# Half of layer 1's modulation by VectorE instead of TensorE, partial sums in a slot

## The chip, the cores and the metric

The kernel runs on one core of one Trainium2 chip. The metric is the device time of one execution in microseconds; where several runs are given, their median.

## The reference

Two layers of a hybrid trunk run over 128 context tokens and 512 latent tokens with 1024 channels, all in fp32. Each layer is a gated feed-forward half-step, a mixer (windowed attention, pooling, short convolution) and a second feed-forward half-step; every one of the three starts from a modulated norm and ends with a gate. Shift, scale and gate of all three come from the modulation:

```python
def ada_params(cond, w_ada, b_ada):
    m = jax.nn.silu(cond) @ w_ada + b_ada          # 1024 -> 9 x 1024, for each layer
    return m.reshape(m.shape[:-1] + (N_MOD, D_MODEL))

def modulated_norm(x, mod, k, g):
    shift, scale = mod[:, None, 3 * k], mod[:, None, 3 * k + 1]
    return rms_norm(x, g) * (1 + scale) + shift

def ffn_sublayer(x, mod, k, g, w_in, w_out):
    h = modulated_norm(x, mod, k, g)
    gt, up = jnp.split(h @ w_in, 2, axis=-1)
    return x + 0.5 * mod[:, None, 3 * k + 2] * ((jax.nn.silu(gt) * up) @ w_out)
```

There are two condition vectors, one for latent and one for context tokens, so a layer's modulation is a product of 2 x 1024 with 1024 x 9216: few operations, but 36 MB of weights for each layer.

## The kernel before, in words

Activations are kept transposed, channels on partitions: eight tiles `xT` of 128 x 640 tokens, treated in two halves of 320. Every big product is done in three matmuls (`mm3`, lines 352 to 354): weights and activations are split into a rounded high part and a remainder (fp32r), and high x high, high x low and low x high are summed in PSUM. The six stages follow one another: (layer, sublayer) = (0, 0), (0, 1), (0, 2), (1, 0), (1, 1), (1, 2); sublayers 0 and 2 are feed-forward (`ffn`), 1 is the mixer.

A feed-forward stage runs over 22 tiles j of 128 hidden channels. Stage (0, 0) uses the plain form (`up`). Stages (0, 2), (1, 0) and (1, 2) use from j = 3 on the fast form (`fast_ups`, `fast_ends`): gate and up products in seven smaller products, numbered 1 to 7, of 12 matmuls each, in the order 1, then 3 and 4 of the j before, then 6, 2, 7, 5. Product 2 alone goes to the PSUM tile `po`. Product 7 of j starts the PSUM tile `c`; VectorE adds it to `gate2` (line 675), and product 4 of the same j, issued within the next j, then accumulates onto `c`. The weights for that are prepared in `fast_weights`: four additions by VectorE (line 646, into the two `sums` tiles) and four splits, each a copy by ScalarE (`wh`, line 170) and a subtraction by VectorE (`wl`, line 176). After j = 6, 11 and 15 a `down` multiplies a chunk of hidden tiles `g` by the second matrix; the last chunks follow after the loop.

All weights come through a ring of five tiles `raw` of 512 KB, loaded in order by SyncE's queue (SP). The tiles of the activations (`h`, `g` and others) are taken from one pool of 22 slots.

The modulation is done beside the feed-forward stages, in 18 chunks of 512 columns for each layer. `side` (line 1286), called after each j, advances a generator `ada_steps(l, c, vector)` by a number of steps that `spread` works out; a chunk has five steps, the first four each with a load of 512 KB of `w_ada` into a `raw` tile, the last with the closing work. `budget` (line 1335) gives 14 chunks (4 to 17 of layer 0) to stage (0, 0), 11 chunks (0 to 10 of layer 1) to (0, 2) and 7 chunks (11 to 17 of layer 1) to (1, 0). So stage (0, 2) does 55 steps over 20 values of j, (1, 0) does 35 over 20.

`ada_steps` has two ways. With `vector` false, each step issues 8 matmuls (`ada_matmuls`, line 275) with the condition in 32 columns as weights and 128 x 128 of `w_ada` as moving data, four column strips side by side; the PSUM tile `mis` is held for all five steps. With `vector` true, each step multiplies the loaded rows by the condition as a per-partition scalar and adds them up on VectorE (lines 309 and 311), for two conditions; at the end 8 matmuls with `pick` (line 319) add over the partitions. Both end with `add_bias`: a copy to `arow` by VectorE (line 264), a transpose by TensorE (line 265) and an addition (line 266). Before, `vector` is true for all of stage (0, 0) and false elsewhere.

The order on each engine's queue is laid out at build time by a planner, which takes the ready instruction of highest priority, where priority follows the order of the program, and gives out buffers as they come free. On the chip each engine runs its queue in that order.

Of the kernel before, what the change touches and what calls it, by code (L numbers as in the profile page):

```python
# [96 lines left out]
def trunk_kernel(ctx: ExitStack, tc: tile.TileContext, i: dict, o: dict):  # L97
# [16 lines left out]
    def mis():  # L114
        return mis_p.tile([P, 512], F32, tag="mis", name="mis")

    def slot(dt=F32, name="slot", shape=(2, T)):
        return slots.tile([P, *shape], dt, tag="slot", name=name)
# [23 lines left out]
    def raw_tile():  # L142
        return rawp.tile([P, 1024], F32, tag="raw", name="raw")

    def sum_tile(name="sums"):
        return sump.tile([P, 1024], F32, tag="sums", name=name)

    def load_ada(l, ci, q, tile):
        src = i["w_ada"][l, q * 256 : (q + 1) * 256, ci * 512 : (ci + 1) * 512]
        nc.sync.dma_start(tile, src.rearrange("(k p) c -> p k c", p=P))  # L150
        return tile
# [110 lines left out]
    def add_bias(l, ci, ps, row):  # L262

        nc.vector.tensor_copy(row, ps[:, 0:P])
        nc.tensor.transpose(ps[:, P : 2 * P], row, ident)
        nc.vector.tensor_tensor(
            mods[l][:, ci * 4 : ci * 4 + 4, :],
            ps[:, P : 2 * P].rearrange("p (g j) -> p g j", g=4)[:, :, 0:2],
            bcol[l][:, ci * 4 : ci * 4 + 4].unsqueeze(2).to_broadcast([P, 4, 2]),
            op=ALU.add,  # L270
        )

    def ada_matmuls(ps, r, q, k):
        for g in range(4):
            last = nc.tensor.matmul(  # L275
                ps[32 * g : 32 * g + 32, 0:P],
                c2[:, 2 * q + k, :],
                r[:, k, g * P : (g + 1) * P],
                start=(q + k == 0),
                stop=(q + k == 4),  # L280
            )
        return last
# [10 lines left out]
    def ada_steps(l, ci, vector):  # L293

        row = lambda: small.tile([P, P], F32, tag="sq", name="arow", bufs=3)
        if vector:
            part = sum_tile().rearrange("p (j c) -> p j c", j=2)
        else:
            ps = mis()
        for q in range(4):  # L300
            r = load_ada(l, ci, q, raw_tile().rearrange("p (k c) -> p k c", k=2))
            for k in range(2):
                if not vector:
                    ada_matmuls(ps, r, q, k)
                    continue
                for j in range(2):
                    c = c2[:, 2 * q + k, j : j + 1]
                    if q + k == 0:
                        nc.vector.tensor_scalar_mul(part[:, j, :], r[:, k, :], c)
                    else:  # L310
                        nc.vector.scalar_tensor_tensor(  # L311
                            part[:, j, :], r[:, k, :], c, part[:, j, :], op0=ALU.mult, op1=ALU.add
                        )
            yield
        if vector:
            ps = mis()
            for j in range(2):
                for g in range(4):
                    nc.tensor.matmul(
                        ps[32 * g : 32 * g + 32, 0:P],  # L320
                        pick[:, j, :],
                        part[:, j, g * P : (g + 1) * P],
                        start=(j == 0),
                        stop=(j == 1),
                    )
        add_bias(l, ci, ps, row())
# [4 lines left out]
    def gain(l, n, half):  # L331

        if half == 0:
            gains[l][n] = const.tile([P, KD, 2], F32, name=f"gain{l}{n}")
        a = gains[l][n][:, half * 4 : half * 4 + 4, :]
        c = (3 * n + 1) * 8 + half * 4
        g = gcol[:, (l * 3 + n) * 8 + half * 4 : (l * 3 + n) * 8 + half * 4 + 4]
        nc.vector.scalar_tensor_tensor(
            a, mods[l][:, c : c + 4, :], 1.0, g.unsqueeze(2).to_broadcast([P, 4, 2]), op0=ALU.add, op1=ALU.mult
        )  # L340

    def gate(l, n):
        g = mods[l][:, (3 * n + 2) * 8 : (3 * n + 3) * 8, :]
        if n != 1:
            t = const.tile([P, KD, 2], F32, name=f"gate{l}{n}")
            nc.vector.tensor_scalar_mul(t, g, 0.5)
            g = t
        gates[l][n] = g
# [23 lines left out]
    def norm_head(hf):  # L372
        a, b = HALVES[hf]
        ps = mis()
        nc.tensor.matmul(ps[:, :HALF], ones, ssq[:, a:b], start=True, stop=True)
        return rsqrt_newton(ps[:, :HALF], eps_d)
# [173 lines left out]
    def shift_products(gate, up):  # L550
# [3 lines left out]
        return bias, last  # L554

    def ffn(l, f, n, hs, side, finish, nxt, first=None):
        w_in = i["w_ffn_in"][l, f]
        w_out = i["w_ffn_out"][l, f]
# [151 lines left out]
        if first:  # L710
            first(gated)
        else:
            ups_by_half(0, 2)
            side(1)
        for j in range(2, NJ):
            if first or j < PLAIN:
                up(j)
            else:
                ends = fast_ups(j, ends)
            side(j)  # L720
            if ch < len(FF_CHUNKS) - 2 and j == FF_CHUNKS[ch][1] + (2 if first else 1):
                down(ch)
                ch += 1
# [15 lines left out]
    def load_mixer_constants():  # L739
        nc.sync.dma_start(edge, i["edge"].rearrange("p (t e) -> p t e", t=2))  # L740
        nc.sync.dma_start(pair, i["pair"])
        nc.sync.dma_start(sinkb, i["sink"].unsqueeze(0).to_broadcast([P, DEPTH, NH]))
        bcol.append(load_rows(72, (nc.sync, slice(0, 72), i["b_ada"][1].rearrange("(r c) -> r c", c=P))))
        gains_qk = [(nc.sync, (slice(16 + x, 18 + x), slice(h * HD, h * HD + HD)), i[w])
                    for x, w in ((0, "q_norm_g"), (2, "k_norm_g")) for h in range(2)]
        c = load_rows(
            20,
            (nc.sync, slice(0, 4), i["pool_scale"].rearrange("l (t p) -> (l t) p", p=P)),
            (nc.sync, slice(4, 16), i["conv_w"].rearrange("l k (t p) -> (l k t) p", p=P)),
            *gains_qk,  # L750
        )

        nc.vector.tensor_scalar_mul(qgs, c[:, 16:18], -0.5)
        nc.vector.tensor_scalar_mul(kg, c[:, 18:20], -4.0)
        pcol.append(c)
# [460 lines left out]
    hs = Plain()  # L1216
# [67 lines left out]
    running, held = [], []  # L1284

    def side(steps, vector):

        for _ in range(steps):
            if not running:
                l, c = todo.pop(0)  # L1290
                if (l, c) == (0, 8):
                    load_mixer_constants()
                running.append((l, c, ada_steps(l, c, vector)))
            l, c, g = running[0]
            with tc.issue_after(held.pop()) if held else nullcontext():
                done = next(g, running) is running
            if done:
                running.pop()
                n, what = divmod(c // 2, 3)
                if what == 1:  # L1300
                    gain(l, n, c % 2)
                elif what == 2 and c % 2:
                    gate(l, n)

    def spread(count, j0, vector):

        n, count = NJ - 1 - j0, count * 5
        return lambda j: side((j - j0 + 1) * count // n - (j - j0) * count // n, vector) if j0 <= j < NJ - 1 else None
# [26 lines left out]
    budget = {(0, 0): 14, (0, 2): 11, (1, 0): 7}  # L1335
    for x, (l, n) in enumerate(steps):
        last = x == len(steps) - 1
        fast = not last and steps[x + 1][1] != 1
        new = Seven() if fast else Plain()
        if last:  # L1340
            nxt = output
        else:
            heads = []

            def nxt(hf, t):
                if t < KD - 1:
                    return
                heads.append(norm_head(hf))
                if hf == 1 and fast:
                    seven(*steps[x + 1], new, heads)  # L1350
                elif hf == 1:
                    for h in range(2):
                        norm_tail(*steps[x + 1], h, new, heads[h])

        finish = nothing if last else squares
        if n == 1:
            mixer(l, hs, finish, nxt)
        else:
            ffn(l, n // 2, n, hs, spread(budget.get((l, n), 0), 1 if x else 4, x == 0), finish, nxt, None if x else first_tiles)
        hs = new  # L1360


# [28 lines left out]
```

## Time and profile before

| | us |
|---|---|
| median of three runs | 2360.88 (2357.27 to 2363.95) |
| profiled execution, own time | 2359.89 |
| its span, first to last instruction | 2358.1 |
| TensorE busy | 2302.1 (98%) |
| VectorE busy | 1526.2 (65%) |
| ScalarE busy | 1055.0 (45%) |
| GpSimd busy | 123.9 (5%) |

In the profile's rows PE is TensorE's matmuls, PEld its weight loads, DVE VectorE, ACT ScalarE, POOL GpSimd, SP SyncE; L352 is line 352 of the kernel. `acc<-h,wh` names the written tile and the read ones. Busy time is the union of an engine's instructions; a matmul's row lasts from its start to its modelled end, and the next one starts long before that, so the distance from start to start tells more than the duration. One fp32 matmul of the program stands as two instructions in the trace. The stages lie about at: (0, 0) to 530 us, mixer to 755, (0, 2) to 1216, (1, 0) from 1250 to 1640, mixer to 1912, (1, 2) to the end.

### The profile page before, as it was taken

The page shows a single profiled execution, that of the slowest core. Times are in us where ns is not written, and L with a number is a line of the kernel's source. Part 1 is how long each engine was busy: PE and PEld are TensorE (multiplying, and loading weights), DVE is VectorE, ACT ScalarE, POOL GpSimd, SP SyncE. Part 2 cuts the span into 40 slices and gives each one's busy share as a digit, 9 for nine tenths or more (in the row PEclk, how much of TensorE's full clock was granted, in tenths as well). Part 3 has the DMA queues.
Part 4 walks back from the last instruction along what each step waited for, and adds up shares of the span by engine and source line. Part 5 has one row for each costly group of instructions (what it writes and reads, how often), then busy time and mean ns, then how long its engine had stood idle before and what let it go on. Part 6 is the DMA issues. An engine that isn't in the chain of part 4 may idle for free.

```text
span 2358.1 us, 40880 instructions
## 1 busy us (share of the span) xinstructions
PE 2302.1 (98%) x16594; PEld 2220.2 (94%) x16594; DVE 1526.2 (65%) x3133; ACT 1055.0 (45%) x1852; POOL 123.9 (5%) x157
## 2 busy tenths in 40 slices
PE   7899999999999999999999999999999999999999
PEld 6899999998978999999999999999898789999999
DVE  5546665556767756666667576675658676666674
ACT  4423233335767534343455343343556674344351
POOL 2101010001200000000000000000111000000000
PEclk9999999999999999999999999999999999999999
DMA  8858596727533544453544333433475242322321
GB/s 274 213 141 230 160 263 165 198 64 159 133 86 81 144 142 127 117 164 100 158 98 126 117 115 109 134 106 112 90 163 115 54 91 79 106 73 85 89 81 45
DMA packets 355988, 301.04 MB, mean 128 GB/s; under 512 B 27384, under 2 KB 303192, under 8 KB 355800
## 3 DMA queue, kind: packets, MB, share of 16 engines
q1 hardware_dynamic: 340932, 244.88, 34.5%
q0 software_dynamic: 14688, 53.48, 12.5%
q8 instruction: 130, 2.13, 0.4%
q14 instruction: 58, 0.48, 0.1%
q10 hardware_dynamic: 180, 0.07, 0.0%
HBM read 242.04 MB, written 2.88 MB: 104 GB/s over the span
## 4 chain that ended last, share of the span: by engine, by line
PE 82%; issue 7%; DMA 5%; DVE 4%; ACT 2%; POOL 0%; SPq 0%; ACTq 0%; POOLq 0%; DVEq 0%
PE acc L352 21%; PE acc L353 21%; PE acc L354 21%; PE mis L353 3%; PE mis L352 3%; PE mis L354 3%; DMA wl<-raw 2%; PE mis L275 2%; PE po L352 1%; DMA raw<-in_w_ffn_in 1%; PE po L353 1%; PE po L354 1%; DMA raw<-in_w_ada 1%; PE acc L1060 1%; PE mis L1111 1%
## 5 line engine op out<-in xcount | busy, mean ns | idle before, releaser
L352 PE MATMUL acc<-h,wh 128*128 128x320 f32 (+1 forms) x2808 | 878.2, 315 | 17.4 <-ACT h L416 5.4
L354 PE MATMUL acc<-h,wl 128*128 128x320 f32 (+1 forms) x2808 | 870.7, 311 | 10.5 <-DMA wl<-raw 10.5
L353 PE MATMUL acc<-h,wh 128*128 128x320 f32 (+1 forms) x2808 | 872.9, 312 | 4.5 <-DVE h L412 3.9
L170 ACT ACTIVATE wh<-raw 128x1024 fp32r<-128x1024 f32 (+2 forms) x332 | 306.2, 924 | 653.0 <-PE mis L353 289.8
L352 PEld LDWEIGHTS acc<-h,wh 128*128 128x128 f32 x2808 | 530.7, 190 | 33.1 <-issue 8.1
L354 PEld LDWEIGHTS acc<-h,wl 128*128 128x128 f32 x2808 | 531.3, 189 | 13.7 <-DMA wl<-raw 13.5
L353 PEld LDWEIGHTS acc<-h,wh 128*128 128x128 f32 x2808 | 531.7, 189 | 6.7 <-DVE h L412 4.1
L176 DVE TENSOR_TENSOR wl<-raw,wh 128x1024 fp32r<-128x1024 f32 (+2 forms) x228 | 222.2, 975 | 58.9 <-ACT wh L170 54.5
L352 PE MATMUL acc<-g,wh 128*128 128x320 f32 x832 | 258.2, 310 | 0.0
L353 PE MATMUL acc<-g,wh 128*128 128x320 f32 x832 | 258.0, 310 | 0.0
L354 PE MATMUL acc<-g,wl 128*128 128x320 f32 x832 | 257.3, 309 | 0.0
L170 ACT ACTIVATE wh<-sums 128x1024 fp32r<-128x1024 f32 x114 | 120.2, 1059 | 199.9 <-PE acc L353 90.7
L176 DVE TENSOR_TENSOR wl<-sums,wh 128x1024 fp32r<-128x1024 f32 x114 | 139.4, 1224 | 71.7 <-ACT wh L170 53.4
L174 POOL DMA_DIRECT2D wl<-raw x102 | 89.5, 877 | 1734.2 <-DVE x L518 967.8
L518 DVE SCALAR_TENSOR_TENSOR x<-acc,gate,x 128x128 f32<-128x128 f32 (+1 forms) x352 | 125.2, 394 | 84.5 <-PE acc L354 82.8
L353 PE MATMUL mis<-g,wh 128*128 128x320 f32 x576 | 177.9, 309 | 0.0
L354 PE MATMUL mis<-g,wl 128*128 128x320 f32 x576 | 177.8, 309 | 0.0
L352 PE MATMUL mis<-g,wh 128*128 128x320 f32 x576 | 177.8, 309 | 0.0
L352 PEld LDWEIGHTS acc<-g,wh 128*128 128x128 f32 x832 | 156.3, 188 | 1.8 <-issue 1.6
L354 PEld LDWEIGHTS acc<-g,wl 128*128 128x128 f32 x832 | 156.4, 188 | 0.2
L353 PEld LDWEIGHTS acc<-g,wh 128*128 128x128 f32 x832 | 156.3, 188 | 0.3
L311 DVE SCALAR_TENSOR_TENSOR sums<-raw,c,sums 128x512 f32<-128x512 f32 x196 | 135.2, 745 | 26.1 <-DMA raw<-in_w_ada 25.8
(208 smaller groups left out, 3177.1 us busy)
## 6 DMA issues: line engine op xcount, KB each, us to landing
raw<-in_w_ffn_in SPq DMA_DIRECT2D x176, 512.0 KB, 3.9
raw<-in_w_ada SPq DMA_DIRECT2D x128, 512.0 KB, 4.9
wl<-raw POOLq DMA_DIRECT2D x102, 512.0 KB, 5.5
raw<-in_w_ffn_out SPq DMA_DIRECT2D x48, 512.0 KB, 5.0
raw<-in_w_ffn_out SPq DMA_DIRECT2D x64, 320.0 KB, 3.8
raw<-in_w_in SPq DMA_DIRECT2D x20, 512.0 KB, 5.5
adaw<-in_w_ada SPq DMA_DIRECT2D x16, 512.0 KB, 9.7
raw<-in_w_in SPq DMA_DIRECT2D x16, 256.0 KB, 6.5
```

The lines of the kernel that those rows point to most:

```text
L170: nc.scalar.activation(h, raw, AF.Copy)
L174: nc.gpsimd.dma_start(lo, raw, accum_op=ALU.add)
L176: eng.tensor_tensor(lo, raw, f32(h), op=ALU.subtract)
L275: last = nc.tensor.matmul(ps[32 * g : 32 * g + 32, 0:P], c2[:, 2 * q + k, :], r[:, k, g * P : (g + 1) * P], start=(q + k == 0), stop=(q + ...
L311: nc.vector.scalar_tensor_tensor(part[:, j, :], r[:, k, :], c, part[:, j, :], op0=ALU.mult, op1=ALU.add)
L352: nc.tensor.matmul(out, wh, xh, start=start, stop=False, skip_group_check=onto)
L353: nc.tensor.matmul(out, wh, xl, start=False, stop=False, skip_group_check=onto)
L354: return nc.tensor.matmul(out, wl, xh, start=False, stop=stop, skip_group_check=onto)
L518: nc.vector.scalar_tensor_tensor(xT[t][:, s:e], ps[:, s - a : e - a], gates[l][n][:, t, j : j + 1], xT[t][:, s:e], op0=ALU.mult, op1=ALU.add,)
L1060: nc.tensor.matmul(ps[:, :w], qs[2 * c + m][:, g, self.qc], self.kk[x][:, g, :], start=(x == 0), stop=(x == 1),)
L1111: nc.tensor.transpose(pt[:, (g * 2 + m) * P : (g * 2 + m + 1) * P], self.pr[m][:, g, x * P : (x + 1) * P], ident,)
```

## The change

`spread` gets a function of the chunk's number instead of a constant: stage (0, 0) stays true for every chunk (x is 0), the other stages are true for odd chunks. So the nine chunks 1, 3, ..., 17 of layer 1 go the `vector` way, five of them in stage (0, 2), four in (1, 0); the nine even ones stay on TensorE. The partial sums, 128 x 1024 in fp32, are taken from the pool of slots and no longer from the `sums` tiles, which `fast_weights` uses in the fast stages; that holds for stage (0, 0) too.

```diff
         if vector:
-            part = sum_tile().rearrange("p (j c) -> p j c", j=2)
+            part = slot(name="apart", shape=(2, 512))
         else:
             ps = mis()
...
-                running.append((l, c, ada_steps(l, c, vector)))
+                running.append((l, c, ada_steps(l, c, vector(c))))
...
-            ffn(l, n // 2, n, hs, spread(budget.get((l, n), 0), 1 if x else 4, x == 0), finish, nxt, None if x else first_tiles)
+            ffn(l, n // 2, n, hs, spread(budget.get((l, n), 0), 1 if x else 4, lambda c, x=x: x == 0 or c % 2 == 1), finish, nxt, None if x else first_tiles)
```

## Rows read from the trace of the kernel before

**Rows 1.** The page: busy us and share by engine; the chain that ended last, by engine.
```profile
PE 2302.1 (98%) x16594; PEld 2220.2 (94%) x16594; DVE 1526.2 (65%) x3133; ACT 1055.0 (45%) x1852; POOL 123.9 (5%) x157
...
PE 82%; issue 7%; DMA 5%; DVE 4%; ACT 2%; POOL 0%; SPq 0%; ACTq 0%; POOLq 0%; DVEq 0%
```
**Rows 2.** Busy time by stretch: from:to, length, busy of each engine, clock, DMA share, GB/s.
```profile
130.00:480.00 350.00, 349.14 (x2520) 343.07 (x2519) 215.63 (x450) 111.19 (x165) 25.32 (x30) 1.00 0.72 190
755.00:1216.00 461.00, 457.04 (x3611) 445.02 (x3611) 296.93 (x536) 188.30 (x310) 3.28 (x4) 1.00 0.44 131
1216.00:1250.00 34.00, 30.84 (x236) 28.66 (x235) 28.46 (x67) 28.31 (x57) 3.46 (x4) 1.00 0.70 171
1250.00:1640.00 390.00, 389.87 (x2940) 382.35 (x2939) 259.03 (x432) 158.90 (x253) 1.73 (x2) 1.00 0.40 117
2059.30:2071.60 12.30, 12.30 (x85) 12.30 (x85) 9.82 (x16) 6.80 (x12) 0.00 (x0) 1.00 0.24 69
```
**Rows 3.** Line 275: duration ns min/median/max, first, last; its first and last stretch (timeline).
```profile
L275 PE MATMUL mis<-raw,c x1152: 272/273/297, 764.0 to 1607.7; 128*32 128x128 f32 x192
...
764.01 0.62 PE L275 MATMUL mis<-raw,c 128*32 128x128 f32 x10
...
1607.34 0.64 PE L275 MATMUL mis<-raw,c 128*32 128x128 f32 x16
```
**Rows 4.** Timeline of TensorE around one stretch of 32: start us, us, instruction, count.
```profile
1295.58 0.31 PE L354 MATMUL acc<-h,wl 128*128 128x320 f32 x1
1295.82 1.08 PE L275 MATMUL mis<-raw,c 128*32 128x128 f32 x32
...
1297.08 0.30 PE L353 MATMUL acc<-h,wh 128*128 128x320 f32 x1
```
**Rows 5.** Timeline of TensorE around one stretch of `pick` products, stage (0, 0).
```profile
243.01 0.31 PE L354 MATMUL acc<-h,wl 128*128 128x322 f32 x1
243.25 0.65 PE L319 MATMUL mis<-sums,pick 128*32 128x128 f32 x16
...
244.08 0.31 PE L353 MATMUL acc<-h,wh 128*128 128x320 f32 x1
```
**Rows 6.** VectorE, lines 311 and 309: groups (busy us, mean ns, idle before), then two timeline rows.
```profile
L311 DVE SCALAR_TENSOR_TENSOR sums<-raw,c,sums 128x512 f32<-128x512 f32 x196 | 135.2, 745 | 26.1 <-DMA raw<-in_w_ada 25.8
...
L309 DVE TENSOR_SCALAR sums<-raw,c 128x512 f32<-128x512 f32 x28 | 12.4, 480 | 9.9 <-DMA raw<-in_w_ada 9.9
...
205.01 5.39 DVE L311 SCALAR_TENSOR_TENSOR sums<-raw,c,sums 128x512 f32<-128x512 f32 x8 [1.35 <-DMA raw<-in_w_ada]
...
215.18 0.87 DVE L309 TENSOR_SCALAR sums<-raw,c 128x512 f32<-128x512 f32 x2
```
**Rows 7.** Timeline of VectorE, then of TensorE, in one j of stage (1, 2).
```profile
2062.26 1.23 DVE L176 TENSOR_TENSOR wl<-sums,wh 128x1024 fp32r<-128x1024 f32 x1 [0.51 <-ACT wh L170]
...
2066.93 0.48 DVE L675 TENSOR_TENSOR part<-acc,part 128x320 f32<-128x320 f32 x1
...
2068.11 0.31 PE L352 MATMUL acc<-h,wh 128*128 128x320 f32 x1
...
2070.16 0.31 PE L354 MATMUL acc<-h,wl 128*128 128x320 f32 x1
...
2071.64 0.31 PE L352 MATMUL po<-h,wh 128*128 128x320 f32 x1
```
**Rows 8.** Waits, 130 to 480 us, then 755 to 1216: total us, times, longest us.
```profile
DVE sums L311 <- DMA raw<-in_w_ada: 19.8, 8, 5.7
...
DVE sums L646 <- DMA raw<-in_w_ffn_in: 38.6, 16, 4.9
...
PEld mis L265 <- DVE arow L264: 2.9, 4, 1.6
...
PE mis L265 <- DVE arow L264: 1.9, 2, 1.4
```

## The prediction

> **What bounds the kernel now.** I read the page's totals and its chain first, then busy time by stretch, then the added and removed instructions one by one, and last the waits. The totals give TensorE 98% of the span and the chain puts 82% of it on TensorE [rows 1]; an average can hide a stage with another limit, so the two stages that change are read alone. The edit of `spread` acts in two stretches: the feed-forward stage (0, 2), about 755 to 1216 us, which carries chunks 0 to 10 of layer 1's modulation, and stage (1, 0), about 1250 to 1640 us, which carries chunks 11 to 17. TensorE is busy 457.0 of 461 us in the one and 389.9 of 390 us in the other; VectorE 297 (64%) and 259 (66%) [rows 2]. So TensorE work that leaves these stages shortens them by its own length, as long as VectorE stays out of TensorE's way. The whole question is whether it does.
>
> **What leaves TensorE.** A chunk of modulation is 32 matmuls of the program; the trace has 1152 for 18 chunks, so 64 instructions for each [rows 3]. Their mean duration (273 ns) must not be multiplied by the count: four of them, one for each 32-column strip, run side by side and successive ones overlap. What counts is by how much a stretch of them delays the next big matmul. A stretch of 32 stands between big matmuls at 1295.58 and 1297.08: 1.50 us for two steps, where two ordinary steps take 0.29 (24 steps from 2068.11 to 2071.64, [rows 7], are 0.147 each), so it costs 1.21 us [rows 4]. A stretch of 16 small matmuls of the same shape, the `pick` products of stage (0, 0), stands between 243.01 and 244.08: 1.07 less 0.29 is 0.78 us [rows 5]. From the two, each small matmul costs 0.027 us and each entry and exit together 0.35 us. The 1152 lie in 45 stretches, the first at 764.01 and the last at 1607.34 [rows 3], 2.5 for each chunk: 64 x 0.027 + 2.5 x 0.35 = 2.60 us. Nine chunks (1, 3, ..., 17) lose this: 23.4 us. Each gets one stretch of 16 `pick` products back, 9 x 0.78 = 7.0 us. The transpose and the bias stay. TensorE's work falls by 16.4 us; five chunks (9.1 us) in stage (0, 2) and four (7.3 us) in stage (1, 0).
>
> **What VectorE gets.** A chunk adds 2 tensor-scalar and 14 scalar-tensor-tensor operations of 128x512. One of the latter lasts 745 ns and one of the former 480 [rows 6], but eight in a row took 5.39 us: (5.39 - 0.745) / 7 = 0.664 us from start to start, and two of the former 0.87 us. So a chunk is 14 x 0.664 + 0.87 = 10.2 us, and the nine are 92 us. VectorE rises to (297 + 51) / 461 = 75% and (259 + 41) / 390 = 77%: room on average.
>
> In detail it is tighter. Between two `down` products, one j of the fast form takes TensorE 12.3 us, in which VectorE is busy 9.8 [rows 2]. Stage (0, 2) does 55 steps over 20 values of j, so a chunk of five steps lasts 1.82 j. During an odd chunk VectorE then needs 1.82 x 9.8 + 10.2 = 28.0 us while TensorE offers 1.82 x 12.3 + 0.78 = 23.2: it falls 4.8 us behind. In stage (1, 0), with 35 steps, a chunk lasts 2.86 j: 38.2 against 36.0, 2.2 us behind. The even chunk that follows gives back 7 us or more (1.82 x 12.3 + 2.6 = 25.0 against 17.8), and so does each `down`. What covers the lag is VectorE's lead: the low part of the tile for product 6 is ready at 2063.49 (2062.26 + 1.23) and first read at 2070.16 (the third of the twelve matmuls ahead of the `po` group, which starts at 2071.64), 6.7 us later [rows 7]. 4.8 fits into 6.7. One operation has no such lead: adding product 7 to `gate2` ends at 2067.41 and product 4, 24 matmuls ahead of the `po` group, writes the same PSUM tile from 2068.11, 0.70 us later [rows 7]. An added operation in front of it (0.664 us) just fits. The engines' orders are fixed beforehand by priorities that follow the program, where this addition precedes the chunk's work, so more than one in front is not the rule.
>
> The Trainium skill (VectorE: DVE Perf Modes, The DRAIN you can't avoid) says that the next operation does not start until the pipe of the one before has emptied, which speaks against the change: at 745 ns for each a chunk would be 11.4 us and the lag 6.0 instead of 4.8, nearly all of the 6.7. The trace does not agree: 0.664 from start to start. The sum stays with the row.
>
> So VectorE's cost to TensorE lies between 0 (the lead covers all) and 5 x 4.8 + 4 x 2.2 = 33 us (nothing is covered). The nearest rows: in stage (0, 0), with 14 chunks by this very path, TensorE was idle 0.9 of 350 us [rows 2], though there VectorE does not split the weights of the up-projections; in stage (0, 2), TensorE waited 2.9 + 1.9 us in 11 chunks for the copy `arow` that VectorE makes at a chunk's end, 0.4 us a chunk, at 64% load [rows 8]. With the load at 76% I take 0.5 us a chunk, 4.5 us.
>
> **What costs nothing or next to it.** The loads are the same, 36 of 512 KB. Their raw tiles come free when VectorE has read them instead of when TensorE has, which can be earlier or later; SyncE's queue behind them holds the next j's weights. VectorE already waited 38.6 us in 16 waits for those in stage (0, 2) without TensorE idling more than 4 us [rows 2, 8]. In stage (0, 0) only the buffer of the partial sums changes, from two of `sums`, which nothing else uses there, to one of 22 slots. In the fast stages the count of slots is tight and enough: 14 operand tiles, at most 7 of `g` and one of sums. If it were not, the chunk would wait for a `down`, and its result is wanted one stage later. The PSUM tile of an odd chunk is held for its end alone instead of five steps, which leaves `down` three instead of two; with TensorE at 390 of 390 us that buys nothing. The order of all engines is laid anew, so the turns between stages move; in the turn from 1216 to 1250 us TensorE idles 3.2 of 34 us [rows 2], and I allow 3 us either way.
>
> **The sum.** The profiled execution took 2359.89 us, 1 us under the median of the three runs (its span is 2358.1). 2359.9 - 16.4 + 4.5 = 2348.0; against the median, 2349.
>
> **Rivals.**
> (B) The lag comes through by half: in a j with three steps VectorE has 8 us more to do, and its lead is the lead of the weight buffers, which come free at TensorE's pace. 33 / 2 = 16.5 us take the place of the 16.4: 2360. For it: the 28.0 against 23.2 in stage (0, 2), and that both stages would then have no spare half a microsecond. Against it: 6.7 us of lead, and the three `down` stretches of each stage.
> (C) Slower: VectorE stands at the head of its queue for a raw tile of the modulation, and the `gate2` addition, the splits and the PSUM evacuations behind it wait with it. Before, that wait would have been TensorE's own, late in its order, and never showed. In stage (0, 0) these waits were 19.8 us in 8, 2.5 us each, for 56 tiles [rows 8]. In the fast stages each would cost what exceeds 0.70 us, 1.8 us. Nine such waits eat the gain, thirteen make the kernel slower by over 0.3%; if half of the 36 tiles waited, 18 x 1.8 = 32 us: 2360 - 16 + 32 = 2376. For it: the 16 waits of the weight additions for their loads in stage (0, 2). Against it: at stage (0, 0)'s rate, where the DMA engines are busier (0.72 against 0.44 and 0.40, [rows 2]), it would be 5 waits, 9 us.
>
> **How the numbers follow.** About 0.3% (7 us) is what a measurement of this kernel can tell from no change: faster means under 2353.8, slower over 2368. Forecast 0.60, its own range 2343 to 2354 (from nothing lost and 2 us of present waits gone, to 11 us lost); B 0.27; C 0.13. The range 2342 to 2368 takes in B and leaves C out. Faster 0.60, same 0.27, slower 0.13.
>
> **What would show it.** In the profile of the changed kernel: 576 instead of 1152 instructions of the modulation's products on TensorE from layer 1's loads and 368 instead of 224 of `pick`; VectorE busy 51 and 41 us more in the two stages; the stretch from the first `po` group of stage (0, 2) to its last, and the same in (1, 0), shorter by 6 to 9 us; TensorE's idle time there still under 5 us. I am wrong if TensorE's gaps ahead of product 4 or of the weights' low parts add up to more than 9 us (B), or if VectorE's waits for modulation loads come out more than a dozen and TensorE's gaps follow them (C).

## The result, and the profile after

The changed kernel takes 2392.08 us (median of five runs, 2384.91 to 2393.55) against 2362.08 for the kernel before on the same chip: a ratio of 1.0123, 95% interval 1.0110 to 1.0136. It is slower by 1.2%; I had forecast faster by 0.5%, and the time lies above the whole range. The profiled execution took 2384.91 us, 25.0 more than that of before; it is the fastest of the five.

The instructions are what the diff says. The first two rows are durations of a line (count, ns min/median/max, first and last start in us), the third is VectorE's group of line 311 (busy us, mean ns, idle before it), then follow the page's totals and the chain by engine:

```profile
L275 PE MATMUL mis<-raw,c x576: 272/273/298, 800.1 to 1595.3; 128*32 128x128 f32 x192
...
L319 PE MATMUL mis<-apart,pick x368: 272/273/298, 124.5 to 1633.2; 128*32 128x128 f32 x184
...
L311 DVE SCALAR_TENSOR_TENSOR apart<-raw,c,apart 128x512 f32<-128x512 f32 x322 | 222.5, 743 | 3.3 <-DMA raw<-in_w_ada 3.3
...
PE 2298.3 (96%) x16162; PEld 2217.8 (93%) x16162; DVE 1608.9 (68%) x3277; ACT 1054.5 (44%) x1852; POOL 123.8 (5%) x157
...
PE 75%; issue 8%; DMA 8%; DVE 5%; ACT 3%; POOL 0%; ACTq 0%; POOLq 0%; SPq 0%; DVEq 0%
```

Of the chain TensorE keeps 75% instead of 82%, and DMA rises from 5 to 8% [rows 1]. Neither says where. A cut by stages does. The norm at the start of the next stage ends with a matmul of line 375; I take the start of the last one of each stage as its end (the last stage ends with the span), in the profiled execution of each kernel:

| us | (0, 0) | mixer | (0, 2) | (1, 0) | mixer | (1, 2) |
|---|---|---|---|---|---|---|
| before | 532.2 | 226.5 | 469.2 | 455.8 | 226.5 | 447.8 |
| after | 569.1 | 225.9 | 461.7 | 452.6 | 226.6 | 447.4 |
| difference | +36.9 | -0.6 | -7.5 | -3.2 | +0.1 | -0.4 |

The two stages that got the new path are shorter by 10.7 us together. Stage (0, 0), where the same instructions run on the same engines as before, is longer by 36.9. Busy time by stretch of after (columns as in [rows 2]), the first over the same 350 us of stage (0, 0), the others within the two fast stages:

```profile
130.00:480.00 350.00, 326.55 (x2263) 318.50 (x2264) 198.67 (x410) 101.44 (x146) 24.31 (x28) 0.96 0.69 182
791.00:1245.00 454.00, 450.58 (x3384) 439.60 (x3384) 346.68 (x621) 189.80 (x315) 4.34 (x5) 1.00 0.45 133
1280.00:1663.00 383.00, 379.96 (x2759) 374.61 (x2757) 289.22 (x489) 152.85 (x247) 1.52 (x2) 1.00 0.42 123
```

In stage (0, 0) TensorE now idles 23.5 of 350 us where it idled 0.9 [rows 2], and VectorE is less busy, not more. Its queue shows what is different. VectorE's timeline of before, the first chunk of that stage (start us, us, instruction, count, idle before):

```profile
83.25 0.89 DVE L309 TENSOR_SCALAR sums<-raw,c 128x512 f32<-128x512 f32 x2 [7.09 <-DMA raw<-in_w_ada]
84.04 4.06 DVE L311 SCALAR_TENSOR_TENSOR sums<-raw,c,sums 128x512 f32<-128x512 f32 x6
```

and of after:

```profile
110.65 1.13 DVE L586 SCALAR_TENSOR_TENSOR sg<-acc,bias,sg 128x128 f32<-128x128 f32 x3
111.70 0.48 DVE L309 TENSOR_SCALAR apart<-raw,c 128x512 f32<-128x512 f32 x1
112.09 0.89 DVE L156 TENSOR_TENSOR g<-sg,g 128x320 fp32r<-128x320 f32 x2
112.90 0.48 DVE L309 TENSOR_SCALAR apart<-raw,c 128x512 f32<-128x512 f32 x1
113.29 9.36 DVE L311 SCALAR_TENSOR_TENSOR apart<-raw,c,apart 128x512 f32<-128x512 f32 x14
```

Before, the first product is 28 us earlier, as soon as its rows have landed. After, it stands at the end of a tile j, behind its `sg` and beside its two `g`; all 14 chunks of the stage begin so, where before five of the 14 begin elsewhere. Then up to 16 products come in a row, where it was up to 10.

What that does to TensorE is seen at one gap of stage (0, 0), in five views of after. SyncE's queue, VectorE and ScalarE by timeline, the chain of waits, TensorE by timeline:

```profile
338.21 11.81 SPq L150 DMA_DIRECT2D raw<-in_w_ada  x4
350.11 13.81 SPq L181 DMA_DIRECT2D raw<-in_w_ffn_in  x2
```

```profile
363.63 0.48 DVE L309 TENSOR_SCALAR apart<-raw,c 128x512 f32<-128x512 f32 x1
371.08 0.89 DVE L156 TENSOR_TENSOR g<-sg,g 128x320 fp32r<-128x320 f32 x2 [6.97 <-ACT g L155]
371.89 0.48 DVE L309 TENSOR_SCALAR apart<-raw,c 128x512 f32<-128x512 f32 x1
```

```profile
368.54 1.06 ACT L170 ACTIVATE wh<-raw 128x1024 fp32r<-128x1024 f32 x1 [9.01 <-DMA raw<-in_w_ffn_in]
...
370.60 0.81 ACT L155 ACTIVATE g<-sg 128x320 fp32r<-128x320 f32 x2
```

```profile
358.95 4.55 DMA wl<-raw
363.55 4.96 DMA raw<-in_w_ffn_in
...
368.58 2.50 issue
371.10 4.50 DMA wl<-raw
```

```profile
370.60 0.30 PE L353 MATMUL acc<-h,wh 128*128 128x320 f32 x1
375.64 0.63 PE L354 MATMUL acc<-h,wl 128*128 128x320 f32 x1 [4.73 <-DMA wl<-raw]
...
376.34 0.47 PE L353 MATMUL acc<-h,wh 128*128 128x322 f32 x1
376.61 0.47 PE L354 MATMUL acc<-h,wl 128*128 128x322 f32 x1
```

It is a circle. Four loads of a chunk are issued from 338.21 us and take four of the five `raw` tiles. They are read only from 363.63 on, for VectorE's next step is to wait 6.97 us for ScalarE's copy `g`; this stands in ScalarE's queue behind the copy `wh`, which waits 9.01 us for a load of weights; and that load starts only at 363.55, when the accumulating DMA `wl<-raw` (line 174) gives the one tile back that still goes round. With one tile, load (4.96), issue (2.50) and accumulation (4.50) stand one behind the other, and TensorE idles 4.73 us. The waits of 60 to 530 us, in total, times, longest us, for before:

```profile
ACT wh L170 <- DMA raw<-in_w_ffn_in: 61.1, 10, 10.0
...
ACT sg L585 <- DVE bias L553: 18.8, 4, 7.3
...
PE acc L354 <- DMA wl<-raw: 1.7, 1, 1.7
```

and for after:

```profile
ACT wh L170 <- DMA raw<-in_w_ffn_in: 83.6, 13, 9.0
ACT sg L585 <- DVE bias L553: 82.9, 10, 11.6
...
PE acc L354 <- DMA wl<-raw: 20.3, 9, 4.7
...
PE acc L354 <- DVE wl L176: 7.1, 1, 7.1
```

TensorE's waits for the accumulation grow from 1.7 to 20.3 us. ScalarE's waits for `bias`, which VectorE copies, grow as well (18.8 to 82.9), and TensorE once waits 7.1 us for a split by VectorE; so the changed order reaches TensorE by more ways than the ring.

Last, the gap has a tail. Busy time by stretch of after, ahead of the gap, in it, and behind it (the seventh number is the granted clock):

```profile
360.00:370.00 10.00, 9.03 (x61) 8.77 (x60) 1.69 (x5) 1.43 (x2) 0.00 (x0) 1.00 0.47 107
370.00:376.00 6.00, 1.27 (x8) 1.01 (x7) 4.92 (x9) 1.41 (x3) 0.86 (x1) 0.84 0.46 87
376.00:381.00 5.00, 5.00 (x20) 5.00 (x20) 5.00 (x9) 0.00 (x0) 0.00 (x0) 0.51 0.85 283
381.00:386.00 5.00, 5.00 (x47) 4.61 (x46) 1.53 (x6) 2.16 (x4) 0.00 (x0) 1.00 0.71 241
```

Behind the 4.73 us of idling the granted clock is 0.51, the 1.2 GHz level, and TensorE does 20 matmuls in 5 us while it counts as fully busy; then it is back at 2.4 GHz. From the starts of all of TensorE's matmuls in stage (0, 0): the distances over 0.45 us exceed the ordinary step of 0.147 by 20.3 us before and 47.6 after; the distances of 0.26 to 0.45 us, most of them slow steps, by 6.1 and 13.9. So of the 36.9 us, 27.3 are more gaps and about 7.8 the slow steps that follow them.

### The profile page after: what moved, and what is told of

Its sections match the earlier page's. It is cut to its first block, busy times and chain, and to the rows that moved or that the text cites. A ratio compares the mean times of both kernels' runs of the same rounds, so it can differ in the third digit from the quotient of the medians.

```text
span 2383.1 us, 40139 instructions
## 1 busy us (share of the span) xinstructions
PE 2298.3 (96%) x16162; PEld 2217.8 (93%) x16162; DVE 1608.9 (68%) x3277; ACT 1054.5 (44%) x1852; POOL 123.8 (5%) x157
## 3 DMA queue, kind: packets, MB, share of 16 engines
q0 software_dynamic: 14688, 53.48, 12.3%
## 4 chain that ended last, share of the span: by engine, by line
PE 75%; issue 8%; DMA 8%; DVE 5%; ACT 3%; POOL 0%; ACTq 0%; POOLq 0%; SPq 0%; DVEq 0%
PE acc L352 19%; PE acc L354 19%; PE acc L353 19%; DMA wl<-raw 4%; PE mis L352 3%; PE mis L354 3%; PE mis L353 3%; DMA raw<-in_w_ffn_in 3%; DVE apart L311 2%; PE po L353 1%; PE po L352 1%; PE po L354 1%; PE mis L275 1%; PE acc L1060 1%; PE mis L1111 1%
## 5 line engine op out<-in xcount | busy, mean ns | idle before, releaser
L311 DVE SCALAR_TENSOR_TENSOR apart<-raw,c,apart 128x512 f32<-128x512 f32 x322 | 222.5, 743 | 3.3 <-DMA raw<-in_w_ada 3.3
```

The source lines that it names most:

```text
L311: nc.vector.scalar_tensor_tensor(part[:, j, :], r[:, k, :], c, part[:, j, :], op0=ALU.mult, op1=ALU.add)
```

## The experiments

All ratios are to the kernel before, run on the same chip, with 95% intervals. In the expectations S is the theory that the partial sums' place in the shared pool costs stage (0, 0) its time, R that held `raw` tiles do it, D that VectorE's long runs of products do it, L that the fast stages are limited by VectorE's lead.

**Only stage (0, 0) put back.** The new path in the fast stages stays.

```diff
-            part = slot(name="apart", shape=(2, 512))
+            if l == 0:
+                part = sum_tile().rearrange("p (j c) -> p j c", j=2)
+            else:
+                part = slot(name="apart", shape=(2, 512))
```

> Layer 0's chunks get their partial sums back in the sums tiles; layer 1's odd chunks keep the slot and VectorE. Theory S (the slot: in stage (0, 0) a chunk can start only once the hidden tile g of the same j has its slot, because slots are given out in the order of the program): the 36.9 us that stage (0, 0) gained go away, 532 us again, the fast stages stay at 462 and 453 us; total 11 us under the kernel before, ratio 0.993 to 0.997. Rival V (VectorE's 92 us more in layer 1 reorder everything, stage (0, 0) too): stage (0, 0) stays near 569 us, ratio near 1.012.

2351.85 us against 2362.92: 0.9956 (0.9944 to 0.9968). Stage (0, 0) takes 531.1 us, the fast stages 466.0 and 453.8 in the profiled execution, a little more than theory S had. The whole loss goes with this one edit, and what is left of the change is a gain of 11.1 us.

**Only the slot, nothing else.** Before, with the one line; all of layer 1 on TensorE.

```diff
-            part = sum_tile().rearrange("p (j c) -> p j c", j=2)
+            part = slot(name="apart", shape=(2, 512))
```

> The kernel before with the partial sums in a slot and nothing else; all of layer 1 on TensorE. Theory S: stage (0, 0) takes 569 us as in the changed kernel, the fast stages 469 and 456 as before; total 37 us over the kernel before, ratio 1.014 to 1.018. Rival V: no change, ratio 1.000.

2406.17 us: 1.0191 (1.0173 to 1.0209). Stage (0, 0) takes 572.0, and the wait of its TensorE for the accumulation is that of after:

```profile
PE acc L354 <- DMA wl<-raw: 21.1, 10, 3.5
```

With the old line put back the whole loss is gone, and the new line alone brings all of it: the loss is this edit's. The ratio is a little above what theory S gave (1.014 to 1.018). Of the 43 us between the medians the profiled execution has 39.8 in stage (0, 0) and 5.9 in the second mixer, 232.4 us instead of 226.5, which the edit does not touch; where those 5.9 come from was not followed up.

**Place or order.** Before, with its `sums` tiles; a chunk's first product is only tied behind the last `g` subtraction of the tile j in whose turn the chunk begins.

```diff
-                        nc.vector.tensor_scalar_mul(part[:, j, :], r[:, k, :], c)
+                        with tc.issue_after(gdone[0].ins):
+                            nc.vector.tensor_scalar_mul(part[:, j, :], r[:, k, :], c)
...
+                gdone[:] = [nc.vector.tensor_tensor(gs[j][:, 1, a:b], sg, f32(gs[j][:, 0, a:b]), op=ALU.subtract)]
```

> The kernel before, partial sums in the sums tiles, but each chunk's first product is placed behind the last VectorE operation on the hidden tile g traced before it, as if the slot had to be handed out in order. Theory S (order of the queue is the cause): stage (0, 0) goes to 565 to 575 us, ratio 1.013 to 1.018 although no slot is used. Rival P (the place: a slot's address, or its extra wait on the load that used the slot before): 532 us, ratio 1.000.

2406.94 us: 1.0184 (1.0171 to 1.0197), stage (0, 0) 574.4: the stage as theory S had it, the ratio just above. VectorE's timeline at the first chunk is again that of after, though the sums lie where they lay before:

```profile
114.64 0.49 DVE L596 TENSOR_TENSOR g<-sg,g 128x320 fp32r<-128x320 f32 x1
115.05 0.88 DVE L312 TENSOR_SCALAR sums<-raw,c 128x512 f32<-128x512 f32 x2
115.85 9.36 DVE L314 SCALAR_TENSOR_TENSOR sums<-raw,c,sums 128x512 f32<-128x512 f32 x14
```

So it is not where the sums lie, nor how many slots there are, but the order that VectorE's queue gets.

**The slot, asked for one chunk earlier.** After, with the slot of the next chunk taken when a chunk of stage (0, 0) begins (the first one at the end of the first tiles), by a one-column write of GpSimd.

```diff
+    def take():
+        t = slot(name="apart", shape=(2, 512))
+        nc.gpsimd.memset(t[:, 0, 0:1], 0.0)
+        taken.append(t)
...
+            if l == 0:
+                part = taken.pop()
+                if ci < 17:
+                    take()
```

> The changed kernel, but in stage (0, 0) the slot of each chunk is taken one chunk earlier, by a memset of one column on GpSimd; sums stay in a slot. Theory S: the chunks can run ahead again, stage (0, 0) falls to 532 to 545 us, total 0 to 11 us under the kernel before, ratio 0.995 to 1.002. Rival P: stage (0, 0) stays at 569 us, ratio 1.012.

2351.56 us: 0.9961 (0.9947 to 0.9975); stage (0, 0) 536.1 in the profiled execution. VectorE's timeline:

```profile
83.95 0.88 DVE L321 TENSOR_SCALAR apart<-raw,c 128x512 f32<-128x512 f32 x2 [7.06 <-DMA raw<-in_w_ada]
```

The same pool, the same sums, and the first product is back at 84 us. What tied it was the place of its slot in the sequence of requests to the pool: `g` asks in each j, and a chunk that asks behind the `g` of a j gets its slot behind that `g`, and with it its place in VectorE's queue, at the end of that j.

**Why order costs: held tiles or long runs.** Both on the kernel with the slot only. In the first, two of a chunk's four loads in stage (0, 0) land in the `sums` tiles, which are idle there; in the second, the products for the second condition are left out after the first one, in all chunks of stage (0, 0), a part of the computation.

```diff
-            r = load_ada(l, ci, q, raw_tile().rearrange("p (k c) -> p k c", k=2))
+            own = sum_tile if vector and q % 2 else raw_tile
+            r = load_ada(l, ci, q, own().rearrange("p (k c) -> p k c", k=2))
```

> The slot-only kernel (slot in stage (0, 0), layer 1 on TensorE), but every second load of the modulation in stage (0, 0) lands in one of the two sums tiles, idle there, instead of in the ring of five raw tiles. The chunks stay tied to g. Theory R (late chunks hold raw tiles, so the next j's weights are loaded late): half of the load on the ring is gone, stage (0, 0) falls from 572 to 535 to 555 us, ratio to the kernel before 1.001 to 1.010. Rival D (VectorE's runs of 14 products in front of the bias copies and PSUM evacuations): stage (0, 0) stays at 565 to 575 us, ratio 1.016 to 1.020.

```diff
                 for j in range(2):
+                    if j == 1 and (q + k) % 8 != 0:
+                        continue
```

> The slot-only kernel, but in stage (0, 0) the products of the second condition are left out after the first (9 operations a chunk instead of 16); loads and order of the chunks stay. Theory D (length of VectorE's runs): the loss halves or better, stage (0, 0) at 532 to 552 us, ratio 1.000 to 1.009. Rival R (raw tiles held until the chunk may start): the wait for g, not the run, sets how long the tiles are held, so stage (0, 0) stays at 558 to 570 us, ratio 1.012 to 1.017.

Landing tiles: 2378.64 us, 1.0066 (1.0053 to 1.0080), stage (0, 0) 551.7. Half the products: 2397.32, 1.0141 (1.0125 to 1.0156), stage (0, 0) 563.4. Against the 572.0 of the slot alone and the 532.2 of before, two tiles give back 20.3 of 39.8 us and half of VectorE's work 8.6. TensorE's waits in stage (0, 0), with the two tiles, then with half the products:

```profile
PE mis L320 <- DVE apart L312: 7.4, 3, 5.5
PE acc L353 <- ACT sg L586: 6.4, 2, 6.0
```

```profile
PE acc L356 <- DMA wl<-raw: 22.1, 9, 4.8
```

With two tiles more the wait for the accumulation is gone from the head of the list (2.6 us are left of 21.1), and a wait for VectorE's late products now leads it; with half the products it is as long as ever. By the medians the two tiles give back 28.1 of 43.3 us and half the products 9.4 of 43.3. So held tiles are shown to be half of the loss or more, and VectorE's amount of work the smaller share. The two edits were not run together, and how the rest divides between long runs and late ends of chunks was not taken apart.

**How much more the fast stages take.** The first experiment with every chunk of layer 1 on VectorE, and then with the odd ones in stage (0, 2) and all seven in (1, 0).

```diff
-lambda c, x=x: x == 0 or c % 2 == 1
+lambda c: True
```

> Sums tiles in stage (0, 0), and all 18 chunks of layer 1 on VectorE instead of the nine odd ones. TensorE loses 16 us of work more. Theory L (VectorE's lead of 6.7 us is used up, since no even chunk gives time back; VectorE would need 15.4 us a j in stage (0, 2) against 12.3 to 12.7 offered): gaps of TensorE ahead of the weights' low parts take the 16 us and more in stage (0, 2), total equal to or slower than the kernel with odd chunks, ratio to the kernel before 0.996 to 1.006. Rival (the lead and the three down stretches cover it): 16 us faster still, ratio 0.987 to 0.990.

```diff
-lambda c, x=x: x == 0 or c % 2 == 1
+lambda c, x=x: x in (0, 3) or c % 2 == 1
```

> Sums tiles in stage (0, 0); in stage (0, 2) the odd chunks on VectorE, in stage (1, 0), where a chunk is spread over 2.86 j, all seven. If VectorE's lead is what limits (15.4 us a j needed in stage (0, 2) with all chunks, 13.4 in (1, 0)), stage (1, 0) gives 3 to 5 us more than with odd chunks there (449 to 451 us) and stage (0, 2) stays at 462 to 466: ratio to the kernel before 0.992 to 0.995. If the fast stages are not limited by it but by the order of slots, no more than with odd chunks: 0.995 to 0.997.

All: 2352.75 us, 0.9959 (0.9947 to 0.9972). Nine more chunks off TensorE, 16 us of its work by the prediction's price, bring nothing over the half. Stage (0, 2) takes 470.1 us, as before the change. Its stretch, and TensorE's first wait in it:

```profile
757.00:1224.00 467.00, 454.00 (x3124) 440.97 (x3123) 406.84 (x726) 192.70 (x321) 4.34 (x5) 0.99 0.45 130
```

```profile
PE acc L355 <- ACT wh L170: 6.8, 11, 1.4
```

TensorE idles 13.0 us there (3.4 after), in many waits for weights. The chain ahead of one of them runs through VectorE, product after product and then the weights' split and sums:

```profile
838.25 2.07 DVE apart L314 x3
...
840.73 1.32 DVE apart L314 x2
842.05 1.14 DVE wl L176
843.18 1.20 DVE sums L649 x2
...
846.68 2.02 ACT wh L170 x2
...
848.74 0.42 PE acc L355
```

So VectorE's lag does reach TensorE when no even chunk lies between, though with far less than the expectation's 15.4 us against 12.3 in every j: VectorE is busy 406.8 of 467 us, and TensorE idles 13.0 us in the whole stretch. Stage (1, 0), with fewer steps per j, takes 449.7, 6.1 less than before. Odd chunks first, then all: 2349.90 us against 2363.14, 0.9945 (0.9930 to 0.9961), the lowest ratio of all kernels here, with stages of 462.5 and 451.1; its interval overlaps that of the first experiment, so only its being faster than before is shown.

**Does the tie cost the fast stages too?** The first experiment with layer 1's slots asked for one chunk early.

```diff
-                part = slot(name="apart", shape=(2, 512))
+                part = taken.pop() if taken else slot(name="apart", shape=(2, 512))
         else:
             ps = mis()
+            if l == 1:
+                take()
```

> Sums tiles in stage (0, 0), odd chunks of layer 1 on VectorE, but each one's slot is taken one chunk earlier, when the even chunk before it starts, so that the chunk is not tied to g in the fast stages either. If the tie costs the fast stages too, they lose 3 to 8 us of TensorE's gaps and the ratio to the kernel before is 0.992 to 0.995; if VectorE's total is what counts there, no change against the kernel with sums in stage (0, 0): 0.995 to 0.997.

2355.57 us, 0.9961 (0.9947 to 0.9975): no difference from the first experiment that can be measured, though the edit does what it should: in the profiled executions the odd chunks begin 2 to 55 us earlier than there.

## Why the prediction was wrong

**The step that failed** is the one under what costs nothing: "In stage (0, 0) only the buffer of the partial sums changes, from two of `sums`, which nothing else uses there, to one of 22 slots." I put this at nothing; for the fast stages I counted the slots and asked whether there are enough. The count was not the point; the pool's other customer was. Tied to `g`, the products lost their lead (28 us at the first chunk), and the loads that they read stood in a ring that the weights share. A question beforehand could have pointed at it: the sentences just ahead of that one name the `raw` tiles and SyncE's queue behind the loads; put to stage (0, 0), whose DMA share of 0.72 was the highest and where GpSimd, busy 25.3 us instead of 1.7 to 3.3, accumulates out of `raw` tiles [rows 2], it leads to the ring. The step is worth 36.9 us in the profiled execution of after, and 2406.17 - 2362.92 = 43 us alone by the medians.

**TensorE's work and VectorE's lag** held in stage (0, 2) and less well in (1, 0). The counts came out as said (576 and 368). Forecast for the fast stages was -16.4 + 4.5 = -11.9. Measured, between the medians, are -11.1 with stage (0, 0) put back, -11.4 with the slot asked for early there, and -7.6 with layer 1's slots early too. In single profiles the two stages together give -10.7 (after), -5.2, -4.5 and -5.9 (those three runs); runs of one kernel lie 4 to 12 us apart here, and a single profile settles no less than that.

All profiles together say more: stage (0, 2) takes 469.2 to 471.9 us in the five kernels with all its chunks on TensorE and 461.7 to 466.0 in the five with the odd ones on VectorE; (1, 0) takes 455.1 to 456.6 in five and 452.6 to 454.7 in four. The means differ by 6.3 and 2.1, where 6.6 and 5.3 were forecast. In (1, 0) one wait takes most of what is missing. Before does not have it; the three other runs show it with 3.2, 3.6 and 1.5 us. For after, the wait, then two pieces of the chain ahead of it:

```profile
PE acc L352 <- ACT part L671: 3.0, 1, 3.0
```

```profile
1301.49 2.93 ACT wh L170 x3
...
1305.14 0.33 ACT part L671
```

ScalarE's copy `part`, which empties a PSUM tile, stands behind three copies of weights. This is neither of the two leads that the prediction weighed; why the changed order has it was not taken apart.

Some luck is in the 4.5 us. The 2.9 and 1.9 us of waiting for `arow` [rows 8] that it starts from are the same waits counted twice: 1.9 us are TensorE's matmuls at 828.7 and 1152.0 us, and the weight loads of these two matmuls, at the same times, are most of the 2.9. Read once, 1.9 us in 11 chunks are 0.17 us a chunk and not 0.4; scaled up as there, to 0.2, the forecast would have been about -14.5, further from what came.

TensorE idled 3.4 of 454 and 3.0 of 383 us in the stretches, under the 5 that I had set.

**VectorE's work** was put a tenth too large: 1608.9 - 1526.2 = 82.7 us instead of 92 (47.9 and 34.8 in the two stages instead of 51 and 41). An added operation overlaps its neighbours, whatever kind they are, often on both sides: the 144 new operations last 101.9 us, and 223 more pairs of neighbours overlap than before. The start-to-start price held: 14 in a row took 9.36 us, (9.36 - 0.743) / 13 = 0.663. The Trainium skill (VectorE: DVE Perf Modes, The DRAIN you can't avoid) has the next operation wait for an empty pipe, but its next sentences, which the prediction leaves out, let one that is not held start earlier. The trace agrees with the latter, by 0.663 against a duration of 0.743, though no run here tests what holds an operation; so the section does not speak against the change as the prediction has it.

**Rival B** (the lag eats the gain) is not borne out for the odd chunks, whose medians keep 7.6 to 11.4 us of the gain, and right for all of them: the limit that it names lies between the two, as 13.0 us of TensorE's idling in stage (0, 2) with all chunks show. **Rival C** (VectorE at its queue's head for a raw tile) is refuted: VectorE's waits for modulation loads fell to 3.3 us, three waits, all in stage (0, 0), from 25.8 and 9.9 [rows 6]. That fall is itself a sign of the loss: VectorE no longer waits for those loads because they lie there long before it comes. The slower side did come, but not by either rival, and in a stage that I had held for unchanged; that C's side had a chance of 0.13 is no merit of its mechanism.

## What to carry to other kernels

Where buffers are given out in the order of the requests, as here, a buffer that moves into a shared pool brings its user into that pool's sequence: ask not only whether there are enough buffers but whose request stands ahead, and what waits while it does. Compare stages that "don't change" by their length and by the order of one engine's queue before any sum is made for those that do. A wait that vanishes from an engine (25.8 to 3.3 us here, on line 311) may mean that its data come earlier than it does, and hold their buffers meanwhile.

## What was not expected of the hardware

The price of a gap is more than the gap. Behind 4.73 us without work TensorE was granted 0.51 of its clock, the 1.2 GHz level, for about 5 us, and steps took 0.27 us instead of 0.147; over stage (0, 0) these slow steps added about 7.8 us to 27.3 us of gaps, a good quarter on top. The page's TensorE total (96% busy) does not show them, since slow steps count as busy.
